# Alternating the high and low weight matmuls one by one, with eight and eight after each break

## The chip, the cores and the metric

The kernel runs on one core of a Trainium2 chip. The metric is the time of one execution in device microseconds (us). A profile shows one execution of its own, which is timed too.

## What is computed

Two transformer-like blocks run one after the other on 256 tokens of width 2048, all in float32. Nearly all the work is in matrix products with weights that are read once from memory; cut to those, the reference is:

```python
# first block
proj = rms_norm(x, g_mix) @ w_in              # q, k, v, r, lr, cb, cc, cx, ga, gb
o    = gla_chunked(q, k, v, log_a)            # gated linear attention, 4 heads
y_a  = (rms_norm(o) * silu(r)) @ w_gla_out
y_b  = (cb * conv(cc * cx)) @ w_conv_out
x    = x + (sigmoid(ga) * y_a + sigmoid(gb) * y_b) @ w_o
x    = x + square(relu(rms_norm(x) @ w_ffn_up)) @ w_ffn_down
x    = rms_norm(x)
# second block: a pooling layer, then latent attention
u, gate = rms_norm(x) @ a_w_in
x    = x + ((mean_pools(u) @ a_w_group) * scale * silu(gate)) @ a_w_out
q, k, v = from two latents of width 512, with norms and rotary positions
x    = x + (attention(q, k, v) * silu(gate)) @ b_w_out
```

The products must come out at about float32 precision, though TensorE multiplies at full rate only in a shortened form of it (called fp32r in the kernel).

## The kernel before

**Two parts of each number.** A number a is split into a high part, rounded to the shortened form, and a low part, the rest. A product is then three products: high weight with high and low activation, and low weight with high activation. The activations of a block of 512 features lie in `part` tiles, for each 128 features the 256 tokens' high parts and behind them their low parts. So one matmul with a high weight tile streams 512 columns (both parts) and gives two sums in the two halves of a PSUM bank; one with a low weight tile streams the 256 high columns and adds to the first half. In what follows the first is called **long**, the second **short**.

**Units.** Weights come as blocks of 512 x 512 (1 MB by DMA, tile `raw`). Half a block, 1024 columns of a tile, is a unit. For each unit ScalarE copies `raw` to the high tile `wh`, and VectorE subtracts to get the low tile `wl`. `ensure` does this three units ahead of TensorE. TensorE's work on a unit in `group` is 16 matmuls: 4 slices of 128 features (`k`) times 2 slices of 128 outputs (`f`), each with a long and a short. Each has its own weight load. In `group` the order for one `k` is long, long, short, short, with `f` 0 and 1 in two PSUM banks. 880 of the kernel's 944 units are of this kind.

The other units are written elsewhere: `group` with one weight block (three matmuls of 256 columns for each slice), `group_tok` (three of 512 columns, with weights and activations in exchanged roles) and `narrow`, the two projections `lr` and `kvr`, which have 16 slices in two units and run long, short, long, short.

**Order of the work.** All queues are written out by a program in one order: after each unit `end_unit` steps a list of small tasks (norms, gates, the linear attention, softmax), as far as VectorE and ScalarE are not too far behind by the program's own reckoning. Some of these tasks put matmuls of their own, mostly small fp32 ones into tiles called `misc`, between two units on TensorE. Where no task does that, units follow each other without anything between.

All matmuls but the transposes go through the helper `mm`, line L230 in the profile of before and L233 in the changed program. `act` (L225) and `tt` (L193) are those of ScalarE and VectorE.

Of the kernel before, what the change touches and what calls it, by code (L numbers as in the profile page):

```python
# [18 lines left out]
P = 128  # L19
# [11 lines left out]
AHEAD = 4000.0  # L31
STAGGER = 2
NSLOT = 33
NROW = 12

VEC = {}
# [63 lines left out]
def kernel(  # L100
# [45 lines left out]

    big_places, row_places = deque(range(NSLOT)), deque(range(NROW))

    def slot(name, shape=(P, 4, T), dt=F32):
        return Slot(spool, big_places, "slot", shape, dt, name)  # L150
# [18 lines left out]
    def psum_now(kind, shape):  # L169
        need(lambda: psum_places[kind])  # L170
        return Psum(kind, shape)
# [13 lines left out]
    def elems(a):  # L185
        return math.prod(a.shape[1:])
# [37 lines left out]
        spent["ACT"] += elems(out) / 1.2 + 100  # L224
        nc.scalar.activation(out, a, f, bias=bias, scale=scale, **kw)  # L225

    def mm(out, lhsT, rhs, start, stop):
        n = elems(rhs)
        spent["PE"] += (n / 2.4 if rhs.dtype == F32R else max(n / 0.6, 214.0)) + 2
        nc.tensor.matmul(out, lhsT, rhs, start=start, stop=stop, skip_group_check=True)  # L230

# [1 line left out]
    order = weight_order()  # L233
    units = [(b, half) for b in range(len(order)) for half in range(2)]
    raw_at, split_at = {}, {}
    state = {"unit": 0, "split": 0, "load": 0, "spare": 1}

    def load_to(b):
        while state["load"] <= min(b, len(order) - 1):
# [55 lines left out]
    def defer(fn):  # L295
        def gen():
            fn()
            return
            yield

        return spawn(gen())
# [16 lines left out]
    def next_unit(name, g, kb):  # L318
        u = state["unit"]
        assert order[units[u][0]] == (name, g, kb), (order[units[u][0]], name, g, kb)  # L320
        ensure(u + NLOOK - 1)
        return split_at.pop(u)

    def end_unit():
        state["unit"] += 1
        ensure(state["unit"] + NLOOK - 1)
        for e in ("DVE", "ACT"):
            spent[e] = max(spent[e], spent["PE"] - 1000.0)
        for t in list(tasks):
            if max(spent["DVE"], spent["ACT"]) > spent["PE"] + AHEAD:  # L330
                break
            if t.wake <= state["unit"]:
                t.step()

    class Out:
# [19 lines left out]
        def done(self):  # L355
            self.s.free()

    def group(name, g, rhs, kbs=range(NKB), into=None):

        kbs = list(kbs)
        n = len(kbs)
        if (name, g) in INTER:
            seq = [(sb, i) for i in range(n) for sb in range(2)]
        else:
            seq = [(sb, i) for sb in range(2) for i in range(n)]
        out = Out(2, lambda: slot("out"))
        if n == 1:
            ps = psum_now("main", (P, 4, T))  # L370
            for sb in range(2):
                wh, wl = next_unit(name, g, kbs[0])
                x = rhs(0)
                for k in range(4):
                    for f in range(2):
                        cs = slice(f * P, (f + 1) * P)
                        o = ps[:, 2 * sb + f, :]
                        mm(o, wh[:, k, cs], x[k // 2][:, k % 2, 0, :], k + f == 0, False)
                        mm(o, wh[:, k, cs], x[k // 2][:, k % 2, 1, :], False, False)
                        mm(o, wl[:, k, cs], x[k // 2][:, k % 2, 0, :], False, k == 3)  # L380
                end_unit()
            return ps
        acc = {}
        if seq[1][0]:
            acc = {sb: psum_now("main", (P, 2, 2, T)) for sb in range(2)}
            state["spare"] = 0
        for e, (sb, i) in enumerate(seq):
            if sb not in acc:
                acc[sb] = psum_now("main", (P, 2, 2, T))
            ps = acc[sb]  # L390
            wh, wl = next_unit(name, g, kbs[e // 2])
            x = rhs(i)
            for k in range(4):
                first, last = i == 0 and k == 0, i == n - 1 and k == 3
                for f in range(2):
                    mm(ps[:, f], wh[:, k, f * P:(f + 1) * P], x[k // 2][:, k % 2], first, False)
                for f in range(2):
                    mm(ps[:, f, 0, :], wl[:, k, f * P:(f + 1) * P], x[k // 2][:, k % 2, 0, :], False, last)
            end_unit()
            if i == n - 1:  # L400
                def fold(ps=ps, sb=sb):
                    fs = slice(2 * sb, 2 * sb + 2)
                    if into is None:
                        out.put(lambda s: fold_parts(s[:, fs, :], ps))
                    else:
                        out.put(lambda s: into(ps, fs))
                    ps.done()

                if into is not None:
                    out.make = lambda: 0  # L410
                defer(fold)
        state["spare"] = 1
        return out

    def fold_parts(dst, ps):
        act(dst, ps[:, :, 1, :], AF.Copy)
        add(dst, ps[:, :, 0, :], dst)

    def group_tok(name, g, rhs, kbs=range(NKB)):

        ps = psum_now("main", (P, 2, 512))
        kbs = list(kbs)
        for i, kb in enumerate(kbs):
            for half in range(2):
                wh, wl = next_unit(name, g, kb)
                x = rhs(i)[half]
                for j in range(2):
                    first = i == 0 and half + j == 0
                    last = i == len(kbs) - 1 and half + j == 2
                    for t in range(2):  # L430
                        tk = slice(t * P, (t + 1) * P)
                        mm(ps[:, t, :], x[:, j, 0, tk], wh[:, j, :], first, False)
                        mm(ps[:, t, :], x[:, j, 0, tk], wl[:, j, :], False, False)
                        mm(ps[:, t, :], x[:, j, 1, tk], wh[:, j, :], False, last)
                end_unit()
        return ps
# [219 lines left out]
    for g in range(2):  # L656
        spawn(qk_evac(group("q", g, h), qs, g, "R16"))
# [34 lines left out]
    for g in range(2):  # L692
        spawn(qk_evac(group("k", g, h), ks, g, "R"))
# [136 lines left out]
    for g in range(4):  # L830
        ps = group_tok("v", g, h)
# [4 lines left out]
    for g in range(4):  # L836
        hold = {}
        ps = group("cc", g, h)

        def evac_cc(ps=ps, hold=hold):  # L840
# [4 lines left out]
        ps = group("cx", g, h)  # L845
# [19 lines left out]
        ps = group("cb", g, h)  # L865
# [12 lines left out]
    for g in range(4):  # L878
        ps = group("gb", g, h)
        gt = {}  # L880
        spawn(gate_steps(ps, get("R"), AF.Sigmoid, gt, 0))
        ps = group("conv_out", g, cbu)
# [11 lines left out]
    for g in range(4):  # L894
        ps = group("r", g, h)
# [15 lines left out]
    for g in range(4):  # L911
        ps = group("ga", g, h)
# [4 lines left out]
        ps = group("gla_out", g, op)  # L917
# [24 lines left out]
    def residual(g):  # L942
        def into(ps, fs):
            for part in range(2):
                add(xs[g][:, fs, :], ps[:, :, part, :], xs[g][:, fs, :])

        return into
# [77 lines left out]
    for part in range(4):  # L1025
# [5 lines left out]
        for g in range(4):  # L1031
            ps = group("down", g, hid, range(4 * part, 4 * part + 4), residual(g))
# [49 lines left out]
    for half in range(2):  # L1082
        y = Pair(4)
        for gi in (2 * half, 2 * half + 1):
            pooled = Pair(2)
            for n in range(2):
                ps = group("u", 2 * gi + n, hp)
# [5 lines left out]
            for n in range(2):  # L1093
                ps = group("pgate", 2 * gi + n, hp)
# [3 lines left out]
            for n in range(2):  # L1098
                ps = group("pgroup", 2 * gi + n, pooled, range(2))
# [15 lines left out]
        for g in range(4):  # L1115
            ps = group("pout", g, y, range(4 * half, 4 * half + 4), residual(g))
# [290 lines left out]
    for i, (name, g) in enumerate(MLA):  # L1407
# [8 lines left out]
        else:  # L1416
            ps = group_tok(name, g, cl, [0])
# [134 lines left out]
```

## Time and profile before

| | us |
|---|---|
| median of three runs | 2756.62 (2756.42 to 2758.18) |
| profiled execution, its own time | 2760.01 |
| its span, first to last instruction | 2758.2 |
| TensorE busy | 2745.0 |
| VectorE busy | 1787.0 |
| ScalarE busy | 1346.1 |

The profile is of one execution. PE is TensorE's matmuls and PEld its weight loads; DVE is VectorE, ACT is ScalarE. The end of a matmul is modelled, and matmuls overlap in the pipeline, so the length of a row says little; the distance between the starts of two rows says how long TensorE needed to get from one to the other. The timeline joins equal instructions that follow each other into one row with a count. The chain of waits is followed back from the last instruction to what released it.

### The profile page before, as it was taken

The page shows a single profiled execution, that of the slowest core. Times are in us where ns is not written, and L with a number is a line of the kernel's source. Part 1 is how long each engine was busy: PE and PEld are TensorE (multiplying, and loading weights), DVE is VectorE, ACT ScalarE, POOL GpSimd, SP SyncE. Part 2 cuts the span into 40 slices and gives each one's busy share as a digit, 9 for nine tenths or more (in the row PEclk, how much of TensorE's full clock was granted, in tenths as well). Part 3 has the DMA queues.
Part 4 walks back from the last instruction along what each step waited for, and adds up shares of the span by engine and source line. Part 5 has one row for each costly group of instructions (what it writes and reads, how often), then busy time and mean ns, then how long its engine had stood idle before and what let it go on. Part 6 is the DMA issues. An engine that isn't in the chain of part 4 may idle for free.

```text
span 2758.2 us, 38593 instructions
## 1 busy us (share of the span) xinstructions
PE 2745.0 (100%) x15906; PEld 2399.1 (87%) x15906; DVE 1787.0 (65%) x2119; ACT 1346.1 (49%) x1584; POOL 25.7 (1%) x36
## 2 busy tenths in 40 slices
PE   8999999999999999999999999999999999999999
PEld 7888888888888888888888888888888888899888
DVE  6676666655666666656556556787657676767564
ACT  5644444444554444434344345554534545555663
POOL 0000000000000000000000000000000010000000
PEclk9999999999999999999999999999999999999999
DMA  6534455555555555555555555555555555655344
GB/s 248 179 138 155 171 178 188 194 183 192 190 184 195 211 191 182 199 185 194 186 189 192 184 193 189 192 186 190 189 191 189 186 194 195 204 187 185 122 172 149
DMA packets 73712, 511.69 MB, mean 186 GB/s; under 512 B 8208, under 2 KB 8752, under 8 KB 13248
## 3 DMA queue, kind: packets, MB, share of 16 engines
q1 hardware_dynamic: 72496, 506.94, 52.2%
q8 instruction: 124, 2.03, 0.3%
q10 hardware_dynamic: 1040, 2.29, 0.2%
q14 instruction: 52, 0.43, 0.0%
HBM read 504.99 MB, written 4.21 MB: 185 GB/s over the span
## 4 chain that ended last, share of the span: by engine, by line
PE 98%; ACT 1%; DVE 0%; DMA 0%; issue 0%; SPq 0%; DVEq 0%; ACTq 0%
PE main L230 95%; PE misc L230 2%; DMA raw<-w_q_dram 0%; ACT s L225 0%; ACT wh L225 0%; ACT L225 0%; DVE wl L193 0%; PE misc L1375 0%; DVE cum L683 0%; ACT e L225 0%; SPq L246 0%; ACT pt L225 0%; ACT ls L225 0%; ACT out L225 0%; DVE x L193 0%
## 5 line engine op out<-in xcount | busy, mean ns | idle before, releaser
L230 PE MATMUL main<-part,wh 128*128 128x512 f32 (+1 forms) x7360 | 2278.5, 392 | 7.6 <-ACT wh L225 7.4
L193 DVE TENSOR_TENSOR wl<-raw,wh 128x1024 fp32r<-128x1024 f32 (+1 forms) x946 | 1152.4, 1222 | 928.0 <-ACT wh L225 921.5
L230 PEld LDWEIGHTS main<-part,wl 128*128 128x128 f32 x7200 | 1354.4, 188 | 314.4 <-DVE wl L193 1.8
L225 ACT ACTIVATE wh<-raw 128x1024 fp32r<-128x1024 f32 (+1 forms) x946 | 997.3, 1058 | 1187.5 <-PE main L230 1094.6
L230 PE MATMUL main<-part,wl 128*128 128x256 f32 x7200 | 1430.0, 278 | 0.7 <-DVE wl L193 0.5
L230 PEld LDWEIGHTS main<-part,wh 128*128 128x128 f32 x7360 | 1124.0, 189 | 12.4 <-ACT wh L225 7.6
L193 DVE TENSOR_TENSOR out<-main,out 128x512 f32<-128x512 f32 x164 | 112.1, 684 | 7.3 <-ACT out L225 7.3
L230 PE MATMUL main<-wh,part 128*128 128x512 f32 x320 | 105.4, 400 | 0.0
L225 ACT ACTIVATE out<-main 128x512 f32<-128x512 f32 x164 | 94.7, 578 | 0.0
L193 DVE TENSOR_TENSOR x<-main,x 128x512 f32<-128x512 f32 x128 | 88.0, 688 | 9.9 <-PE main L230 7.7
L230 PEld LDWEIGHTS main<-wh,part 128*128 128x128 f32 x320 | 61.0, 190 | 12.8 <-issue 0.3
L230 PE MATMUL main<-wl,part 128*128 128x512 f32 x160 | 63.0, 394 | 0.0
L225 ACT ACTIVATE part<-out 128x512 fp32r<-128x512 f32 x56 | 33.2, 627 | 50.7 <-DVE out L206 44.2
L193 DVE TENSOR_TENSOR out<-out,R 128x1024 f32<-128x1024 f32 x42 | 51.4, 1225 | 1.3
L225 ACT ACTIVATE Z<-Z 128x1024 f32<-128x1024 f32 x16 | 17.0, 1062 | 42.0 <-DVE Z L193 36.9
L193 DVE TENSOR_TENSOR part<-out,part 128x512 fp32r<-128x512 f32 x56 | 36.1, 687 | 0.5
L230 PEld LDWEIGHTS main<-wl,part 128*128 128x128 f32 x160 | 30.4, 190 | 5.9
L225 ACT ACT_TABLE_LOAD x24 | 30.8, 1283 | 1.5 <-PEq L1541 0.7
L206 DVE SCALAR_TENSOR_TENSOR part<-x,vec,part 128x256 fp32r<-128x256 f32 x64 | 26.8, 479 | 5.4 <-ACT part L225 5.4
L1068 POOL COPY s<-out 128x4 f32<-128x4 f32 x8 | 9.5, 1188 | 2210.1 <-ACT wh L225 1811.6
L230 PEld LDWEIGHTS misc<-Z 128*128 128x128 f32 x240 | 29.0, 191 | 1.0
L225 ACT ACTIVATE part<-x,vec 128x256 fp32r<-128x256 f32 x64 | 27.2, 495 | 2.9 <-DMA x<-xT 2.8
(188 smaller groups left out, 803.0 us busy)
## 6 DMA issues: line engine op xcount, KB each, us to landing
raw<-w_up_dram SPq DMA_DIRECT2D x64, 1024.0 KB, 4.9
raw<-w_down_dram SPq DMA_DIRECT2D x64, 1024.0 KB, 4.8
raw<-w_u_dram SPq DMA_DIRECT2D x32, 1024.0 KB, 4.8
raw<-w_pgate_dram SPq DMA_DIRECT2D x32, 1024.0 KB, 4.9
raw<-w_pout_dram SPq DMA_DIRECT2D x32, 1024.0 KB, 4.9
raw<-w_v_dram SPq DMA_DIRECT2D x16, 1024.0 KB, 4.8
raw<-w_cc_dram SPq DMA_DIRECT2D x16, 1024.0 KB, 4.8
raw<-w_cx_dram SPq DMA_DIRECT2D x16, 1024.0 KB, 4.8
```

Of the source, the lines that this page charges most:

```text
L193: nc.vector.tensor_tensor(out, a, b, op)
L206: nc.vector.scalar_tensor_tensor(out, a, s, b, op0, op1)
L225: nc.scalar.activation(out, a, f, bias=bias, scale=scale, **kw)
L230: nc.tensor.matmul(out, lhsT, rhs, start=start, stop=stop, skip_group_check=True)
L1068: nc.gpsimd.tensor_copy(nx[:, :, 0:d], cur[:, :, 0:d])
```

## The change

`mm` notes whether a matmul came from the weight stream (`stream`) or from elsewhere; the latter sets `broken`. At the start of each unit `group` asks `unit_order` for the order of its 16 matmuls. If nothing came between, the unit alternates: for each `k` and `f` a long and a short, or a short and a long. If something did, the unit runs eight of one kind and then eight of the other, and `broken` is cleared. A counter of breaks picks one of four forms by turns from `SETTLE`: the first number says whether the run starts with the longs (0) or with the shorts (1), the second which kind comes first in the alternating units until the next break. The set `seen` keeps the start flag on the first matmul into each PSUM bank. The same 16 matmuls with the same operands are issued in each unit.

```diff
+SETTLE = ((0, 0), (0, 1), (1, 0), (1, 1))
...
-    def mm(out, lhsT, rhs, start, stop):
+    def mm(out, lhsT, rhs, start, stop, stream=False):
         n = elems(rhs)
+        if not stream:
+            state["broken"] = True
...
+    def unit_order():
+
+
+        kf = [(k, f) for k in range(4) for f in range(2)]
+        if state["broken"]:
+            state["broken"] = False
+            state["breaks"] += 1
+            first = SETTLE[state["breaks"] % len(SETTLE)][0]
+            return [(part, k, f) for part in (first, 1 - first) for k, f in kf]
+        first = SETTLE[state["breaks"] % len(SETTLE)][1]
+        return [(part, k, f) for k, f in kf for part in (first, 1 - first)]
...
-            for k in range(4):
-                first, last = i == 0 and k == 0, i == n - 1 and k == 3
-                for f in range(2):
-                    mm(ps[:, f], wh[:, k, f * P:(f + 1) * P], x[k // 2][:, k % 2], first, False)
-                for f in range(2):
-                    mm(ps[:, f, 0, :], wl[:, k, f * P:(f + 1) * P], x[k // 2][:, k % 2, 0, :], False, last)
+            seen = set() if i == 0 else {0, 1}
+            for part, k, f in unit_order():
+                fs = slice(f * P, (f + 1) * P)
+                if part:
+                    mm(ps[:, f, 0, :], wl[:, k, fs], x[k // 2][:, k % 2, 0, :], f not in seen, False, True)
+                else:
+                    mm(ps[:, f], wh[:, k, fs], x[k // 2][:, k % 2], f not in seen, False, True)
+                seen.add(f)
```

On TensorE, the place where the second long stretch of units starts (about 1075 us in the trace of before, in an FFN up projection), before the change. `misc` is the last small matmul of a norm, `wh` and `wl` are the high and low weight tiles, `part` the activations:

```order
L230 MATMUL main_8756<-part_8221,wl_8717 128x256 x2
L230 MATMUL misc_8801<-dg_8750,ones 128x256
L230 MATMUL main_8756<-part_8407,wh_8741 128x512 x2
L230 MATMUL main_8756<-part_8407,wl_8742 128x256 x2
L230 MATMUL main_8756<-part_8407,wh_8741 128x512 x2
L230 MATMUL main_8756<-part_8407,wl_8742 128x256 x2
L230 MATMUL main_8756<-part_8408,wh_8741 128x512 x2
```

The same place on TensorE in the changed program:

```order
L233 MATMUL main_8756<-part_8221,wh_8716 128x512
L233 MATMUL misc_8801<-dg_8750,ones 128x256
L233 MATMUL main_8756<-part_8407,wh_8741 128x512 x4
L233 MATMUL main_8756<-part_8408,wh_8741 128x512 x4
L233 MATMUL main_8756<-part_8407,wl_8742 128x256 x4
L233 MATMUL main_8756<-part_8408,wl_8742 128x256 x4
L233 MATMUL main_8756<-part_8597,wh_8773 128x512
L233 MATMUL main_8756<-part_8597,wl_8774 128x256
```

The unit after the `misc` matmul runs its eight longs and then its eight shorts (form 0,0); from the next unit on a long and a short alternate, for 253 units without a break.

On TensorE, the place where the first long stretch starts (about 397 us, in a projection that feeds the convolution), in the changed program:

```order
L233 MATMUL main_3181<-part_192,wh_3174 128x512
L233 MATMUL misc_3257<-dg_3209,ones 128x256
L233 MATMUL main_3181<-part_223,wl_3199 128x256 x4
L233 MATMUL main_3181<-part_224,wl_3199 128x256 x4
L233 MATMUL main_3181<-part_223,wh_3198 128x512 x4
L233 MATMUL main_3181<-part_224,wh_3198 128x512 x4
L233 MATMUL main_3281<-part_109,wh_3231 128x512
L233 MATMUL main_3281<-part_109,wl_3232 128x256
```

Here the eight shorts come first (form 1,0), and the alternating units, 238 of them, start with a long. In the whole program 49 units run eight and eight and 831 alternate. The other engines' instructions keep their order.

More of the change, by code (lines that the diff above doesn't have):

```diff
@@ L235 @@
     raw_at, split_at = {}, {}
-    state = {"unit": 0, "split": 0, "load": 0, "spare": 1}
+    state = {"unit": 0, "split": 0, "load": 0, "spare": 1, "broken": True, "breaks": 0}
     def load_to(b):
```

## The prediction

> **What bounds the kernel now.** I read the page first, for the engine that never rests and for the clock, and then the chain that ended last.
>
> ```profile
> span 2758.2 us, 38593 instructions
> PE 2745.0 (100%) x15906; PEld 2399.1 (87%) x15906; DVE 1787.0 (65%) x2119; ACT 1346.1 (49%) x1584; POOL 25.7 (1%) x36
> PEclk9999999999999999999999999999999999999999
> PE 98%; ACT 1%; DVE 0%; DMA 0%; issue 0%; SPq 0%; DVEq 0%; ACTq 0%
> L230 PE MATMUL main<-part,wl 128*128 128x256 f32 x7200 | 1430.0, 278 | 0.7 <-DVE wl L193 0.5
> ```
>
> TensorE is 98% of the chain, its granted clock is full in every slice, and it hardly waits: 0.5 us in all for a low weight tile. So only the spacing of its matmuls can change the time. The chain in order of time says where they stand unbroken (start us, us, what, matmuls):
>
> ```profile
> 397.47 666.01 PE main L230 x3824
> 1075.50 707.81 PE main L230 x4064
> 1818.50 587.98 PE main L230 x3376
> 2650.47 102.79 PE main L230 x592
> ```
>
> These are three long stretches without a wait. They run from the convolution's projections to the first FFN projection, through the FFN, and through the pooling layer, and take 1962 of the 2758 us. Half of their matmuls are **long** (a high weight part, 512 columns) and half **short** (a low part, 256 columns). One long and one short take 2 x 666.01 / 3824 = 348.3 ns; the next two rows give 348.3 as well. Below, a pair is one long and one short, and its price is all that matters. The present order, two long and two short, reads like this in the timeline (start, length, engine, count; lengths are modelled and overlap, so only starts are used):
>
> ```profile
> 1000.62 0.63 PE L230 MATMUL main<-part,wh 128*128 128x512 f32 x2
> 1001.09 0.39 PE L230 MATMUL main<-part,wl 128*128 128x256 f32 x2
> ```
>
> **The change, part one: one long, one short.** The trace of before already has this order in the two narrow projections, which use one long and one short per step, 16 pairs each. First lr, then kvr:
>
> ```profile
> 57.28 0.40 PE L230 MATMUL misc<-part,wh 128*128 128x512 f32 x1
> 57.51 0.28 PE L230 MATMUL misc<-part,wl 128*128 128x256 f32 x1
> 57.63 0.40 PE L230 MATMUL misc<-part,wh 128*128 128x512 f32 x1
> 57.87 0.28 PE L230 MATMUL misc<-part,wl 128*128 128x256 f32 x1
> 57.99 0.40 PE L230 MATMUL misc<-part,wh 128*128 128x512 f32 x1
> ...
> 62.58 0.40 PE L230 MATMUL misc<-part,wh 128*128 128x512 f32 x1
> ```
>
> ```profile
> 2409.57 0.40 PE L230 MATMUL misc<-part,wh 128*128 128x512 f32 x1
> 2409.80 0.28 PE L230 MATMUL misc<-part,wl 128*128 128x256 f32 x1
> 2409.92 0.39 PE L230 MATMUL misc<-part,wh 128*128 128x512 f32 x1
> 2410.15 0.27 PE L230 MATMUL misc<-part,wl 128*128 128x256 f32 x1
> 2410.26 0.40 PE L230 MATMUL misc<-part,wh 128*128 128x512 f32 x1
> ...
> 2414.77 0.39 PE L230 MATMUL misc<-part,wh 128*128 128x512 f32 x1
> ```
>
> Fifteen pairs take 5.30 us in lr, 353.3 ns each, and 5.20 us in kvr, 346.7 ns each. The same instructions in the same order have **two rhythms**, a slow one with a long of 0.24 us in it (57.63 to 57.87) and a fast one whose longs take 0.23. Each holds from the first pair to the last, across the unit boundary in the middle. Against 348.3 ns the slow rhythm costs 5.0 ns a pair and the fast one gains 1.67.
>
> How many pairs are alternated comes from the order of the changed program: of 880 units 831 alternate, which is 6648 pairs, and 49 follow a break and run eight and eight, 392 pairs. The forms take turns at each break, but the lengths between breaks are very unequal: 238 units (from 397 us) follow eight shorts and then eight longs (form 1,0), 253 and 210 (from 1075 and 1818 us) follow eight longs and then eight shorts (form 0,0), and the last 31 follow form 0,1. All other stretches have at most ten. Since nothing stalls inside the long ones, I take it that a stretch keeps the rhythm it was entered with, so three entries decide 701 units.
>
> What matters for an entry is the run it comes out of: shorts for forms 0,0 and 0,1 (535 alternating units, 4280 pairs), longs for 1,0 and 1,1 (296 units, 2368 pairs). The nearest rows of runs of one width are the one-block projections (three 256-column matmuls a step) and the token-major ones (three of 512):
>
> ```profile
> 2515.64 0.40 PE L230 MATMUL main<-part,wh 128*128 128x256 f32 x2
> 2515.88 0.28 PE L230 MATMUL main<-part,wl 128*128 128x256 f32 x1
> ...
> 2519.60 0.40 PE L230 MATMUL main<-part,wh 128*128 128x256 f32 x2
> ```
>
> ```profile
> 114.01 0.62 PE L230 MATMUL main<-wh,part 128*128 128x512 f32 x2
> 114.47 0.39 PE L230 MATMUL main<-wl,part 128*128 128x512 f32 x1
> ...
> 116.73 0.62 PE L230 MATMUL main<-wh,part 128*128 128x512 f32 x2
> ```
>
> Eleven steps in 3.96 us are 120.0 ns a short; four steps in 2.72 us are 226.7 ns a long. A run of shorts thus enters at 0.12 us a short, the late spacing that lr shows before its rhythm repeats (57.87 to 57.99); kvr keeps dropping to 0.11 (2410.15 to 2410.26). So I expect **slow after shorts**. Longs at 0.227 us leave no lateness behind, so **fast after longs**. Both are weak readings, since lr and kvr come out of the same order two by two; the bounds for each are both rhythms. The sum: 4280 x 5.0 = +21.4 us, 2368 x 1.67 = -3.9 us.
>
> **Part two: the 49 units of eight and eight.** A long and a short in runs of their own take 226.7 + 120.0 = 346.7 ns, 1.67 less than now: 392 x 1.67 = -0.7 us. The bounds are 346.7 and 353.3, -0.7 to +2.0 us. A break itself costs now what it will: the first long after one takes long whatever follows.
>
> ```profile
> 1074.91 0.59 PE L230 MATMUL misc<-dg,ones 128*128 128x256 f32 x2
> 1075.15 0.81 PE L230 MATMUL main<-part,wh 128*128 128x512 f32 x2
> 1075.80 0.40 PE L230 MATMUL main<-part,wl 128*128 128x256 f32 x2
> ```
>
> The two longs stand for 0.65 us where 0.47 is usual; that stays, on a long or on a short, and is left out of the sum.
>
> **Part three: the short comes earlier, so its weights must.** In an alternating unit that starts with a short, the low part is needed at once instead of after two longs, 0.47 us later. VectorE delivers it well ahead in the long stretches (the 0.5 us above is all TensorE waited). It can bite at the start, where the third unit waits for both parts:
>
> ```profile
> 14.93 0.73 PE L230 MATMUL main<-part,wh 128*128 128x512 f32 x2 [0.99 <-ACT wh L225]
> 16.18 0.50 PE L230 MATMUL main<-part,wl 128*128 128x256 f32 x2 [0.52 <-DVE wl L193]
> 17.42 1.06 PE L230 MATMUL main<-part,wh 128*128 128x512 f32 x2
> 18.27 0.63 PE L230 MATMUL main<-part,wl 128*128 128x256 f32 x2
> ```
>
> This unit will start with a short, at 16.18, and the two longs it now fits in while waiting come after: 0.47 us, or 0.85 at the pace of 17.42 to 18.27. Behind the waiting matmul are all later ones. Bounds 0 (another wait absorbs it) to 1.7 us (that pace for four longs); I take 0.7. ACT, VectorE and the weight queue keep their order; they have 35% and more idle time.
>
> **Sum:** 21.4 - 3.9 - 0.7 + 0.7 = +17.5 us. The profiled execution took 2760.0 us, 1.8 more than its span and 0.1% over the median of the three runs, 2756.6; the pair prices hold in both, so the forecast is 2756.6 + 17.5 = 2774.1 us.
>
> **The rivals.**
>
> *Slow everywhere* (24%): the slow rhythm is taken out of longs too, as lr took it after an ordinary pair of shorts. 6648 x 5.0 = +33.2: 2789.8 us. Against it stands kvr.
>
> *Fast everywhere* (24%), the one that ends on the other side: a run of one width leaves TensorE in step, and every stretch starts fast as kvr did. 6648 x 1.67 = -11.1: 2745.5 us. The point from which it decides is the share s of slow pairs: 5.0 s = 1.67 (1 - s) at s = 0.25. A single long stretch (1680 to 2024 pairs) is 25 to 30% of the pairs, so one slow stretch is enough to eat the gain.
>
> *The other way round* (11%): fast after shorts, slow after longs: -7.1 + 11.8 = +4.7, 2761.3 us, inside what can be told.
>
> *No effect* (7%): over hundreds of units the alternating order drifts to 348.3 ns, the price of the present order, which is the same after every break. 2756.6 us. Fifteen pairs without any drift speak against it.
>
> *Below both rhythms* (2%): with a load of another kind between every two matmuls each of them keeps only the shortest spacing that its kind has in any row, 226.7 ns for a long (the token-major rows) and 0.11 us for a short (2410.15 to 2410.26). A pair at 337 ns saves 11.6, 77 us in 6648 pairs: 2679 us. No row shows the two together; no pair above takes less than 346.7 ns. The Trainium skill, page "TensorE: Matmul & The Clock Gate", section "Back-to-back issue gap", goes further and gives N / 2.4 + 2.5 ns from one matmul to the next: 325 ns a pair in any order, as an estimate from that page 2602 us for the changed kernel. The trace does not agree with it in any of its orders (348.3, 353.3 and 346.7 ns).
>
> **The numbers.** The forecast case has 32%, the rivals 24, 24, 11, 7 and 2. About 0.2%, 5.5 us, is what can be told from no change. Slower: 32 + 24 = 56%. Faster: 24 + 2 = 26%. Same: 11 + 7 = 18%. The likeliest case's own range is 2770 to 2779, from the bounds of parts two and three. The 8 in 10 range reaches to slow everywhere above and fast everywhere below, with about 2 us for those bounds: 2743 to 2791.
>
> **What would show it.** The chain of the changed kernel should again have one piece for each long stretch; its length over its matmuls gives the rhythm. I expect 353.3 ns a pair from about 1080 and 1820 us on, and 346.7 from 400 to 1060. Wrong would be: 346.7 in the first of these, a rhythm that changes inside a stretch, a third price, or new waits of TensorE for low weight tiles of more than 2 us in all.

## The result

| | before | changed | ratio, 95% interval |
|---|---|---|---|
| median of four runs, us | 2756.52 | 2790.34 | 1.0120 (1.0108 to 1.0132) |
| profiled execution, us | 2760.01 | 2788.79 | |
| its span, us | 2758.2 | 2787.0 | |

The changed kernel is 33.8 us slower by the medians, and 28.8 by the two profiled executions (its own four lie between 2788.79 and 2792.95). The profiled execution of before lies 3.5 us above its median, and its granted clock is 0.50 in two short stretches, from 17 to 20 us and from 2566.8 to 2570.0 us, where that of the change is 1.00; so the medians are the better measure of the difference. The page of the changed kernel's profile still shows TensorE at 100% of the span, at the full granted clock and with next to no waiting for low weight tiles:

```profile
span 2787.0 us, 38558 instructions
PE 2774.3 (100%) x15906; PEld 2413.6 (87%) x15906; DVE 1787.1 (64%) x2119; ACT 1344.0 (48%) x1584; POOL 25.7 (1%) x36
PEclk9999999999999999999999999999999999999999
L233 PE MATMUL main<-part,wl 128*128 128x256 f32 x7200 | 1968.9, 281 | 0.9 <-DVE wl L194 0.9
```

The chain in order of time (start us, us, what, matmuls) has the same unbroken pieces with the same counts as before, each longer:

```profile
397.76 675.52 PE main L233 x3824
...
1085.43 717.93 PE main L233 x4064
...
1838.90 596.40 PE main L233 x3376
```

They give 2 x 675.52 / 3824 = 353.3 ns a pair, 353.3 and 353.3: the slow rhythm in all of them, after either kind of run. They hold 28.05 of the 28.8 us by which the span grew (675.52 + 717.93 + 596.40 against 666.01 + 707.81 + 587.98). In the rest the start gained 2.0 us, the full clock near 2567 us about 1.6 (an estimate, half of 3.2 us), and so the shorter stretches lost some 4.4 us, near the 5.2 that their 1040 pairs at 5.0 ns would be. The timeline shows the entry at 1085 us:

```profile
1085.09 2.18 PE L233 MATMUL main<-part,wh 128*128 128x512 f32 x8
1087.10 1.11 PE L233 MATMUL main<-part,wl 128*128 128x256 f32 x8
1088.05 0.40 PE L233 MATMUL main<-part,wh 128*128 128x512 f32 x1
1088.29 0.28 PE L233 MATMUL main<-part,wl 128*128 128x256 f32 x1
1088.40 0.40 PE L233 MATMUL main<-part,wh 128*128 128x512 f32 x1
...
1088.76 0.40 PE L233 MATMUL main<-part,wh 128*128 128x512 f32 x1
...
1089.11 0.40 PE L233 MATMUL main<-part,wh 128*128 128x512 f32 x1
```

The eight shorts take 0.95 us, 119 ns each. The first alternating pairs are at 1088.05, 1088.40, 1088.76 and 1089.11: 1.06 us for three, 353.3 ns each, from the first one on. To the nanosecond the starts read 234, 117, 241, 120, 236, 113, 233 and then again 117, 241, 120, 236, 113, 233. That is the pattern of lr, one of the two narrow projections. After a run of longs (397 us) they read 227, 113, 233, 117, 241, 120, 236: the same pattern, entered at another point.

### The profile page after: what moved, and what is told of

The parts are those of the page before. It is cut to its first block, busy times and chain, and to the rows that moved or that the text cites. A ratio compares the mean times of both kernels' runs of the same rounds, so it can differ in the third digit from the quotient of the medians.

```text
span 2787.0 us, 38558 instructions
## 1 busy us (share of the span) xinstructions
PE 2774.3 (100%) x15906; PEld 2413.6 (87%) x15906; DVE 1787.1 (64%) x2119; ACT 1344.0 (48%) x1584; POOL 25.7 (1%) x36
## 3 DMA queue, kind: packets, MB, share of 16 engines
q10 hardware_dynamic: 1040, 2.29, 0.2%
## 4 chain that ended last, share of the span: by engine, by line
PE 99%; DVE 0%; DMA 0%; ACT 0%; issue 0%; SPq 0%; DVEq 0%; ACTq 0%
PE main L233 96%; PE misc L233 2%; DMA raw<-w_q_dram 0%; PE misc L1392 0%; DVE wl L194 0%; DVE cum L700 0%; ACT e L226 0%; ACT wh L226 0%; SPq L249 0%; ACT ls L226 0%; DVE x L194 0%; ACT L226 0%; DVE ls L207 0%; DVE out L194 0%; PE misc L1258 0%
## 5 line engine op out<-in xcount | busy, mean ns | idle before, releaser
L233 PE MATMUL main<-part,wh 128*128 128x512 f32 (+1 forms) x7360 | 2510.3, 394 | 6.8 <-ACT wh L226 6.8
L233 PE MATMUL main<-part,wl 128*128 128x256 f32 x7200 | 1968.9, 281 | 0.9 <-DVE wl L194 0.9
L233 PEld LDWEIGHTS main<-part,wh 128*128 128x128 f32 x7360 | 1370.8, 188 | 332.8 <-ACT wh L226 6.8
L233 PEld LDWEIGHTS main<-part,wl 128*128 128x128 f32 x7200 | 1338.2, 189 | 6.0 <-DVE wl L194 1.6
L233 PE MATMUL misc<-Z 128*128 128x64 f32 (+1 forms) x240 | 28.6, 271 | 0.0
```

## The experiments

In all of them only the order inside the 880 units differs; every kernel computes the whole result. `one` stands for alternating slices, long first; `two` for slices in the old order (long, long, short, short). Where a unit has a number, the 880 units are counted from 0 in the order of the program.

### Without the runs: long first, and short first

The first two take the runs of eight away and let all units alternate.

```diff
-        if state["broken"]:
...
-        return [(part, k, f) for k, f in kf for part in (first, 1 - first)]
+        return [(part, k, f) for k in range(4) for f in range(2) for part in (0, 1)]
```

> All 880 units alternate, long first, and no unit runs eight and eight. Theory A (it is the run of one kind ahead of a stretch that brings the slow rhythm): the three long stretches are entered straight from a small fp32 matmul, as one short stretch of the changed kernel was (a first long of 315 ns after attention's transposes, then 117, 233, 117, 231, 112), and that one was fast. So 346.7 ns a pair in the long stretches, 7040 x 1.67 = 11.7 us off 2756.5: about 2745 us. Theory B (alternation is slow from nearly every entry, and kvr was luck): 353.3 ns a pair, 7040 x 5.0 = +35 us: about 2792 us.

Measured: 2775.09 us, 1.0062 (1.0047 to 1.0077). Neither theory has it, since the stretches part ways. The chain of this kernel:

```profile
397.18 662.83 PE main L233 x3824
1072.18 717.97 PE main L233 x4064
1825.47 596.42 PE main L233 x3376
```

The first stretch runs at 346.7 ns a pair, the other two at 353.3. All three are entered in the same way, a long right behind the same kind of small matmul. In the timeline to 10 ns the entries cannot be told apart until the slow one has a long of 0.24:

```profile
396.83 0.59 PE L233 MATMUL main<-part,wh 128*128 128x512 f32 x1
397.25 0.28 PE L233 MATMUL main<-part,wl 128*128 128x256 f32 x1
397.37 0.39 PE L233 MATMUL main<-part,wh 128*128 128x512 f32 x1
397.60 0.28 PE L233 MATMUL main<-part,wl 128*128 128x256 f32 x1
```

```profile
1071.84 0.58 PE L233 MATMUL main<-part,wh 128*128 128x512 f32 x1
1072.26 0.28 PE L233 MATMUL main<-part,wl 128*128 128x256 f32 x1
1072.37 0.40 PE L233 MATMUL main<-part,wh 128*128 128x512 f32 x1
1072.61 0.28 PE L233 MATMUL main<-part,wl 128*128 128x256 f32 x1
```

To the nanosecond the first long takes 425, 420 and 423 ns in the three. In the same kernel a short stretch with a first long of 418 ns (at 1816 us) is fast, so the length of this one long does not decide by itself. Entries that look alike lead to prices that differ by 2% over hundreds of units. The run of eight is thus not the only way into the slow rhythm.

> All 880 units alternate, short first, and no unit runs eight and eight. Theory A: as with the long first, 346.7 ns a pair (the changed kernel has one unit entered this way after attention's transposes, 202, 235, 117, 230, 117, 230 ns), about 2745 us, and at most 1 us more for low weight tiles that are needed at once. Theory B: 353.3 ns a pair, about 2792 us.

The same edit with `(1, 0)`. Measured: 2747.58 us, 0.9962 (0.9948 to 0.9977), **faster than both kernels**, by 0.4% against before. Its chain (the third piece has 36 matmuls fewer than in the chain above):

```profile
395.58 662.83 PE main L233 x3824
1070.40 704.43 PE main L233 x4064
1809.89 578.83 PE main L233 x3340
```

Each long stretch runs at 346.7 ns a pair; of all stretches only three short ones late in the kernel, of 16 pairs each, are slow. To the nanosecond the pattern is a third one, 230, 117, 230, 117, 230, 116, entered through 305, 233, 117, 235. It has the price of the fast rhythm. The number is near that of theory A, which the first of these two kernels contradicts; what it shows is that alternation as such is not slow.

### The old order ahead of the alternation: three slices, and four

```diff
...
+        pairs = 3 if state["broken"] else 0      # and 4 in the other kernel
+        state["broken"] = False
+        return sum(two[:pairs] + one[pairs:], [])
```

> After a break three slices of a unit run in the old order (two long, two short); from the fourth slice on all alternates, long first. In the trace of before the third slice after a break ends with a short of 112 ns, and kvr, which was fast, came after such a slice. Theory A: the exact distance at the entry decides, so 346.7 ns a pair: 2756.5 - 11 = about 2745 us. Theory B: slow here too, about 2790 us.

> After a break one whole unit, four slices, runs in the old order; from the next unit on all alternates, long first. The fourth slice after a break ends with a short of 119 ns, and lr, which was slow, came after such a slice. Theory A (the exact distance at the entry decides): 353.3 ns a pair, 831 units x 8 x 5.0 = +33 us, about 2790 us, though one slice fewer gives the fast rhythm. A theory C, that any two-by-two order ahead is good and only runs of eight are bad, expects about 2745 us here as with three slices.

Measured: 2773.97 us with three, 1.0057 (1.0042 to 1.0072), and 2762.81 with four, 1.0017 (1.0008 to 1.0027). As numbers, both miss, and theory C falls. Stretch by stretch the rule behind the first expectation holds. The chain with three slices, then with four:

```profile
396.75 662.83 PE main L233 x3824
1071.57 717.95 PE main L233 x4064
1825.00 596.41 PE main L233 x3376
```

```profile
397.84 662.84 PE main L233 x3824
1072.83 704.45 PE main L233 x4064
1812.83 596.39 PE main L233 x3376
```

I read the starts just ahead of each stretch to the nanosecond. Old-order slices take turns: one reads 233, 236, 116, 112 ns, the next 233, 231, 113, 119. Every long stretch that began behind the first kind was fast, every one behind the second slow, in both kernels, and the short ones between two breaks follow the same rule wherever nothing else comes between and the clock is full. What I had wrong was that the third slice after a break is always of the first kind: it is at 397 us, but not at 1075 or 1818.

### Five slices at the third break

The rule then says what to do about the last slow stretch with four: one slice more, there alone (unit 597).

```diff
+        n = state["n"] = state.get("n", -1) + 1
+        pairs = 4 if state["broken"] else 1 if n == 597 else 0
```

> As with four slices in the old order after each break, but five at the break that opens the third long stretch (1818 us in the trace of before). In the run with four slices that stretch alternated after a slice that read 231, 114, 120 ns and was slow. If the slice just ahead decides (old-order slices take turns, one ending with a short of 112 ns, the next with 119), the fifth ends with 112 and this stretch alone turns fast: 1680 pairs x 6.67 = 11.2 us less than with four, about 2751.5 us, the other long stretches unchanged at 346.7 ns. If the number of slices or the place matters otherwise, it stays at 353.3 ns and the time at 2763 us.

Measured: 2750.56 us, 0.9977 (0.9968 to 0.9986), and in the chain:

```profile
396.88 662.84 PE main L233 x3824
1071.87 704.45 PE main L233 x4064
1811.87 585.19 PE main L233 x3376
```

The third stretch went from 596.39 to 585.19 us, 11.2 less, and the others stayed, as the rule says. The slice just ahead now reads 234, 235, 116, 113 ns, the first kind.

### Inside a stretch, with no break

```diff
...
+        pairs = {360: 3, 390: 4, 420: 3, 480: 4, 540: 3}.get(n, 0)
+        return sum(runs if n in (450, 510) else two[:pairs] + one[pairs:], [])
```

> All units alternate, long first, without regard to breaks, as in the first of these runs, where the second long stretch was slow throughout. Inside that stretch, where nothing interrupts the stream, old-order slices are put in at units 360 (three), 390 (four), 420 (three), 480 (four) and 540 (three), and units 450 and 510 run eight and eight. If the entry decides and the break itself does not matter, the rhythm changes inside the stretch: fast, 346.7 ns, wherever the last old-order slice ended with a short of about 112 ns, slow, 353.3 ns, wherever it ended with about 119, and slow after both units of eight and eight. If the rhythm belongs to the stretch or its place in the kernel, it stays slow from 1071 us on.

`runs` is a unit of eight longs and then eight shorts. The view by windows of 80 us between the inserted places (us, busy time and count of TensorE, of weight loads, VectorE, ScalarE, GpSimd, then clock and DMA). The count of matmuls, which includes about two at the edges, is about 454 at 353.3 ns a pair and 463 at 346.7:

```profile
1076.00:1156.00 80.00, 80.00 (x454) 69.39 (x453) 51.06 (x51) 37.51 (x43) 0.00 (x0) 1.00 0.51 185
1161.00:1241.00 80.00, 80.00 (x464) 69.93 (x463) 44.14 (x43) 30.78 (x31) 0.00 (x0) 1.00 0.55 194
1245.00:1325.00 80.00, 80.00 (x463) 69.93 (x462) 52.80 (x52) 37.70 (x44) 0.00 (x0) 1.00 0.50 182
1328.00:1408.00 80.00, 80.00 (x454) 69.36 (x454) 45.51 (x45) 29.68 (x28) 0.00 (x0) 1.00 0.54 189
1414.00:1494.00 80.00, 80.00 (x455) 69.38 (x454) 48.93 (x47) 36.31 (x42) 0.00 (x0) 1.00 0.52 189
1498.00:1578.00 80.00, 80.00 (x455) 69.43 (x454) 46.83 (x46) 31.45 (x31) 0.00 (x0) 1.00 0.53 189
1583.00:1663.00 80.00, 80.00 (x455) 69.32 (x454) 48.49 (x48) 35.39 (x40) 0.00 (x0) 1.00 0.50 181
1667.00:1747.00 80.00, 80.00 (x464) 69.96 (x463) 53.88 (x59) 41.57 (x54) 0.00 (x0) 1.00 0.55 197
```

| put in | short just ahead, ns | rhythm behind it |
|---|---|---|
| nothing yet | | slow |
| three old slices | 112 | fast |
| four | 113 | fast |
| three | 119 | slow |
| a unit of eight and eight | 120 | slow |
| four | 120 | slow |
| a unit of eight and eight | 120 | slow |
| three | 113 | fast |

Three slices turn the rhythm over, four keep it, and both units of eight and eight, which were put in where it was slow, left it slow: all seven places came out as the first outcome says. VectorE and ScalarE are as busy in fast windows as in slow ones, the share of the DMA lies between 0.50 and 0.55 in both, and the clock is 1.00 in all. So neither a break nor the place in the kernel decides, but the point of its own pattern at which TensorE is when the alternation starts. Its time, 2769.07 us, is of a single execution.

### What the runs themselves cost

```diff
...
+        return [(part, k, f) for part in (0, 1) for k in range(4) for f in range(2)]   # eight and eight in every unit
+        return [(part, k, f) for part in ((0, 1), (1, 0))[n % 2] for k in range(4) for f in range(2)]   # sixteen
```

> Every unit runs eight longs and then eight shorts. If a run costs what its steady part costs (226.7 + 120.0 ns a pair, the price in the forecast), a unit takes 2773 ns against 2787 of before: -11.7 us in 880 units, about 2745 us. If each change of kind has its price (the one unit of eight and eight of the changed kernel that follows no break reads 234, 235, 229, 232, 231, 227, 226, 227, 113, 120 ... and takes 2792 ns), it is +5 ns a unit: about 2761 us.

> Units run eight and eight with the kind that comes first taking turns, so runs are of sixteen and there are half as many changes of kind. If each change back and forth costs 2792 - 2773 = 19 ns, two units take 2 x 2773 + 19, 2783 ns each: -3.7 ns x 880 = -3.2 us, about 2753.5 us. If a run costs its steady part alone, 2745 us as with runs of eight.

Measured: 2761.03 us with runs of eight, 1.0015 (1.0006 to 1.0025), and 2753.63 with runs of sixteen, 0.9990 (0.9980 to 0.9999): in each case the expectation that charges for the change of kind. The timeline of the kernel with eight:

```profile
1501.65 2.00 PE L233 MATMUL main<-part,wh 128*128 128x512 f32 x8
1503.49 1.11 PE L233 MATMUL main<-part,wl 128*128 128x256 f32 x8
1504.44 2.00 PE L233 MATMUL main<-part,wh 128*128 128x512 f32 x8
```

A unit takes 2.79 us; eight longs take 1.84 us, 230 ns each instead of 226.7, since the first five of a run take longer (233, 236, 228, 233, 231 ns), and the shorts take 0.95 us.

### One run, and runs followed by three old slices

```diff
...
+        if n == 330:
+            return [(part, k, f) for part in (0, 1) for k in range(4) for f in range(2)]
+        return [(part, k, f) for k in range(4) for f in range(2) for part in (1, 0)]
```

> The fast kernel of these runs (all units alternate, short first, no runs), with one single unit, the one that opens the second long stretch, run eight and eight. If a run of one kind sets the rhythm of all that follows until the next break, the 253 units behind it (2024 pairs) go from 346.7 to 353.3 ns and this one unit costs 13.5 us: 2747.6 + 13.5 = about 2761 us. If the slow rhythm needs more than one run, or short first is proof against it, the cost is that of the unit alone, under 0.1 us: 2747.6 us.

Measured: 2762.56 us, 1.0019 (1.0009 to 1.0028). The chain beside that of the kernel without this one run:

```profile
396.84 662.83 PE main L233 x3824
1071.65 717.93 PE main L233 x4064
1824.85 578.83 PE main L233 x3340
```

The second piece grew from 704.43 to 717.93 us, by 13.5; the other two did not change. The medians differ by 15.0 us; 1.3 of the other 1.5 us come ahead of the first long stretch, where the two programs are the same. One unit's order costs 0.5% of the kernel's time, and that in the stretch behind the unit.

The last kernel is the change itself with three old slices behind each run, and with the long first in all alternating units (in the three long stretches the change has that too):

```diff
...
+            state["next"] = 3
...
+        pairs, state["next"] = state["next"], 0
+        return sum(two[:pairs] + one[pairs:], [])
```

> The change as it is, with its run of eight and eight after each break, but three slices in the old order behind each run before the units alternate, long first. Three old-order slices turned slow into fast inside a stretch (units 360 and 540 of the earlier run). If a run leaves TensorE always at the same point, one rhythm follows in all stretches that it opens: fast if it is the point that the slow rhythm was at, so about 2746 to 2750 us against 2790 of the change; if the point differs between runs that end with longs and with shorts, the first long stretch (ends with longs, 1904 pairs) and the other two (shorts, 3704 pairs) part ways: about 2760 us with the first slow, 2772 us with the others slow. If a run's harm is not in the entry, it stays near 2790 us.

Measured: 2760.90 us, 1.0013 (1.0004 to 1.0023), 29.4 less than the change:

```profile
396.49 675.51 PE main L233 x3824
1084.11 704.44 PE main L233 x4064
1823.89 585.20 PE main L233 x3376
```

The stretch whose run ends with longs is slow, the two whose runs end with shorts are fast. This was one of the stated outcomes, not the one named first. The run's own time is still in the kernel; the two stretches that turned fast are 13.5 and 11.2 us shorter than in the change.

## Why the prediction was right and where it was wrong

The direction was right and the time lies inside the stated range, but the measured +33.8 us is nearly twice the forecast +17.5. The case that came true is the rival "slow everywhere", whose 2789.8 us stand beside 2790.3 measured. The range held because it was drawn out to that rival. The likeliest case's own range, 2770 to 2779 us, is wider than the bounds named for it: they give 16.8 to 21.2 us, or 2773.4 to 2777.8.

**What held.** TensorE's spacing alone decided. The two rhythms and their prices, 353.3 and 346.7 ns a pair, taken from 16 pairs each, hold over hundreds of units, and a stretch keeps the rhythm that it was entered with. "No effect" and "below both rhythms" fall: no long stretch of any kernel ran below 346.6 ns a pair. The 325 ns by the Trainium skill's formula ("TensorE: Matmul & The Clock Gate", "Back-to-back issue gap", where it is called the gap of an isolated matmul) were not seen in any order.

**The step that failed** is "longs at 0.227 us leave no lateness behind, so fast after longs". The first long stretch, 1904 pairs, cost 675.52 - 666.01 = +9.5 us where the forecast had -3.2, and the small stretches behind runs of longs went the same way. Most of the gap of 16.3 us between +17.5 and +33.8 is this term, 12.7 us in this stretch alone. The spacing ahead of the entry was the right thing to look at, but a reading to 10 ns could not tell the point in the pattern. "Slow after shorts" held in size as well: 717.93 - 707.81 = +10.1 us and 596.40 - 587.98 = +8.4 us, as 5.0 ns a pair say. Its reason did not: the late 0.12 us of the shorts is not what parts slow from fast, since runs of longs led into the slow rhythm too, so here the forecast was right in part by luck.

**Part two**, -0.7 us for the 49 units, took the steady price of a run. With eight and eight in every unit a unit takes 2.79 us (1501.65 to 1504.44), no less than the 2.79 of the old order (8 x 348.3 ns), because the first longs after shorts are late. To the nanosecond the units of eight and eight at 1085 and 397 us take 2967 and 2981 ns, and those in the old order at the same two places took 2970. The term is about nothing.

**Part three**, +0.7 us for the start, is not decided by these two executions. The third unit starts with its short at 15.36 us after waiting for it, later than its first long did before (14.93), as expected:

```profile
15.36 0.39 PE L233 MATMUL main<-part,wl 128*128 128x256 f32 x1 [0.75 <-DVE wl L194]
```

But the clock behind it differs. The windows for the same time of before and of the change (columns as above, the clock third from the end):

```profile
17.00:20.00 3.00, 3.00 (x12) 2.61 (x11) 1.18 (x2) 2.01 (x4) 0.00 (x0) 0.50 1.06 421
```

```profile
17.00:20.00 3.00, 3.00 (x20) 2.63 (x19) 2.06 (x4) 3.00 (x6) 0.00 (x0) 1.00 1.05 414
```

The granted clock was 0.50 there before and is 1.00 now, and TensorE does 20 matmuls in these 3 us instead of 12. (The page gives the clock by slices of 69 us, which hide this.) The eighth unit starts at 29.34 us instead of 31.32: 2.0 us gained. That the change's order did this is not shown. Two kernels of the experiments, the one that alternates everywhere with the long first and the one with slices put in inside a stretch, have the same order up to unit 360, and yet their windows differ in the same way:

```profile
17.00:20.00 3.00, 3.00 (x19) 2.58 (x18) 1.51 (x3) 2.59 (x6) 0.00 (x0) 1.00 1.06 415
```

```profile
17.00:20.00 3.00, 3.00 (x11) 2.54 (x11) 1.51 (x3) 2.55 (x5) 0.00 (x0) 0.55 1.06 418
```

So the clock at the start can differ between executions of one and the same order, and what makes it fall stays open.

## What to carry to other kernels

Where matmuls of two lengths share a saturated TensorE, price an order by its repeating pattern, read over many repeats, not by single distances; the same instructions can settle into patterns that differ by 2%. Then look at what comes just ahead of each long stretch, because one unit there can cost more than all it does itself. Here the short first without any settling unit was the best order found: 2747.58 us.

## What was not expected of the hardware

TensorE kept a rhythm of its own for up to 718 us: the same alternation ran at 346.7 or 353.3 ns a pair, and entries a few ns apart led into the one or the other (a first long of 425 ns into the fast rhythm, of 420 and 423 into the slow one, and of 418 into the fast one again), with other engines equally busy and the clock the same. The slow pattern repeats after three pairs, the fast one after two, and a third of the same price after one pair to within a nanosecond. A run of eight shorts, and a run of eight longs, led into the slow one wherever the alternation followed directly, with no wait and no other matmul between. The runs of each kernel that ran more than once agree within 0.2%, and a single long stretch in the other rhythm would move them by 0.4 to 0.5%, so these choices do not seem to change from one execution to the next. Runs of one length cost 226.7 and 120.0 ns a matmul, and together exactly the price of the fast rhythm, but the longs only from about the sixth after a change of kind (233, 236, 228, 233, 230, 227, 227 ns in the changed kernel's run at 397 us). What in TensorE makes the two rhythms stayed open; the runs show the entry that leads into each, not the mechanism.
